# Three steps per head pair in place of four, with row maxima ahead of older steps' values, and filling counted over steps

## The chip, the cores and the metric

The kernel runs on one core of a Trainium2 chip. The time is that of one execution on the device, in microseconds; the time of a kernel is the median of several runs. One further execution is recorded by the hardware profiler, and every row of the profile comes from that one.

## The reference

A trunk of two layers on a sequence of S = 512 tokens, D = 1024. Layer 0 mixes with forgetting attention (FoX, 16 heads of 64), layer 1 with latent attention (MLA, 8 heads of 128 + 64 rotary), whose keys and values are computed once from the stream after layer 0. An MLP of width 4096 with a squared ReLU follows each, and a normalisation closes the trunk. All is float32. The two attentions share this causal softmax in blocks of 128 queries:

```python
def one_block(args):
    i, qb = args
    logits = logits_fn(qb)          # FoX: q.k*scale + cum_q - cum_k; MLA: nope part + rotary part
    qpos = i * Q_BLOCK + jnp.arange(Q_BLOCK)
    logits = jnp.where(kpos[None, :] <= qpos[:, None], logits, -jnp.inf)
    p = jax.nn.softmax(logits, axis=-1).astype(v.dtype)
    return jnp.einsum('bhqk,bkhd->bqhd', p, v)

x = x + ctx.reshape(B, S, W) @ w_out
x = x + sq_relu_mlp(rms_norm(x, norm_ffn_g[layer]), w_up, w_down)
```

## The kernel before

Every float32 operand is split into a rounded high part and a remainder, and each product is three matmuls (high·high, high·low, low·high; `three`, line 260). A weight piece of 512 KB comes by DMA on SP's queue (`fetch`), ScalarE (ACT) casts it to `whi`, VectorE (DVE) subtracts to `wlo` (`piece`, line 250: it prepares the piece asked for and the next one).

Both attentions go through `attention` (line 415). It takes two heads at a time: 8 pairs in FoX, 4 in MLA. A pair has four steps, one for each block of 128 queries, the longest first: blocks 3, 2, 1, 0 with 512, 384, 256 and 128 key columns. A step n does the following, in the order in which the code issues it.

- `start(p)` at a pair's first step: the pair's projection must have been issued; in FoX the table `nb` of forget sums for this pair is loaded on SP's queue (line 577).
- `scores` (line 587 for FoX, 1094 for MLA): TensorE writes the scores of the two heads to two `sc` banks. FoX heads have 64 rows each, so head 0 uses rows 0 to 63 and head 1 rows 64 to 127, and their matmuls alternate; MLA has three matmuls on 128 rows for each head and then three on 64 rows for each. In FoX DVE adds the causal mask to a 128-column part of `nb`.
- `soft_step` (line 379): DVE takes row maxima (a reduction that also writes the tile `t`), ACT the exponentials with their row sums, DVE a reciprocal and two multiplies.
- SKEW = 3 steps later the step's tiles are turned (`turn_unit`, line 405): TensorE transposes them to a `tp` bank, ACT copies to `pth`, DVE subtracts to `ptl`. After a pair's last step `values` multiplies with the values, head by head.
- `fill.run(12)` after each step (9 in MLA), and `fill.run(18)` between the values of the two heads (6 in MLA), hand out other matmuls for TensorE: the later pairs' projections (`proj`, line 499, to `acc` banks, then DVE `t<-acc,rstd`, ACT `r<-t`, DVE `r<-t,r`), the remaining values (`v4_gen`, line 561) and the beginning of the output projection (`out_begin`, line 451). The numbers are FILL1 and FILL2 (lines 34, 35); the Filler (line 347) draws pieces from generators until n are used up, and forgets what a piece took beyond n. `until(key)` draws all up to that piece.

In the attentions a scheduler at build time takes the instructions in about this order, each as its inputs and buffers allow, and writes one fixed sequence for each engine. In the MLPs the order is the written one. Nearly all instructions go through one helper, so the profile puts them on line 112; they are told apart by the names of their tiles.

## Time and profile before

| | us |
|---|---|
| median of 3 runs (1128.93 to 1130.05) | 1128.96 |
| profiled execution | 1129.98 |
| its span | 1127.8 |
| TensorE (PE) busy | 1112.5 |
| VectorE (DVE) busy | 778.8 |
| ScalarE (ACT) busy | 582.3 |

The span is the time from the first to the last recorded instruction. FoX's attention lies at about 52 to 234 us, MLA's at about 651 to 745 us of it; the MLPs between and behind them. A timeline row is the start, the length, engine, line, operation, output<-inputs, rows, then output<-input shapes and how many like it follow each other; in square brackets how long the engine was idle ahead and who released it. Matmuls overlap in the pipeline, so lengths add up to more than the time: from one start to the next is what counts. `MATMUL tp<-ident,t` are transposes, `sc<-r,r` scores, `tp<-pth,v` values, `acc<-r,whi` and `acc<-r,wlo` the filling. `CUSTOM_DVE_ANT_0 t<-sc,nb` is the reduction to row maxima.

### The profile page before, as it was taken

Reading aid. Unit: us, or ns where it says so; the run is one execution under the profiler, and the core shown is the slowest. Engines: PE = TensorE matmul, PEld = TensorE weight load, DVE = VectorE, ACT = ScalarE, POOL = GpSimd, SP = SyncE. Lnnn points to the kernel's source line nnn. Section 1 sums busy time; section 2 is a strip of 40 time slices with the busy share of each in tenths; the row PEclk is TensorE's granted clock in tenths of the full one; section 3 lists DMA queues with packets and bytes.
Section 4 is the critical chain, followed back from the end, with each engine's and each line's share of the span. In section 5 each row is a group of like instructions: output and inputs, shape, how many; then the busy total and the mean of one; then the engine's idle time right before and its main releaser. Section 6 shows DMA issues by size and latency. Waiting matters only on the chain.

```text
span 1127.8 us, 14208 instructions
## 1 busy us (share of the span) xinstructions
PE 1112.5 (99%) x5324; PEld 910.0 (81%) x5324; DVE 778.8 (69%) x1422; ACT 582.3 (52%) x1067; POOL 13.0 (1%) x46
## 2 busy tenths in 40 slices
PE   8999999999999999999999999999999999999997
PEld 6878887788888888888888877888888888888885
DVE  6897788765476667576896878736265765765784
ACT  5565565544555455434444767634575544444622
POOL 1000000001000000000000000000000000000000
PEclk9999999999999999999999999999999999999999
DMA  5423212133634415321345212213442511611402
GB/s 189 132 82 104 78 61 90 57 131 112 246 127 131 131 38 158 105 63 36 125 132 155 75 50 75 94 56 107 154 170 74 186 57 57 200 57 43 131 1 75
DMA packets 37109, 116.92 MB, mean 104 GB/s; under 512 B 4384, under 2 KB 5024, under 8 KB 37040
## 3 DMA queue, kind: packets, MB, share of 16 engines
q1 hardware_dynamic: 36176, 114.41, 31.1%
q10 hardware_dynamic: 864, 1.60, 0.4%
q8 instruction: 42, 0.69, 0.3%
q14 instruction: 27, 0.22, 0.1%
HBM read 109.67 MB, written 6.33 MB: 103 GB/s over the span
## 4 chain that ended last, share of the span: by engine, by line
PE 95%; DVE 2%; ACT 1%; DMA 1%; issue 0%; SPq 0%; ACTq 0%
PE up L112 35%; PE acc L112 20%; PE go L112 19%; PE sc L112 8%; PE tp L112 7%; PE keep L112 6%; DVE t L112 1%; ACT t L112 1%; DVE r L112 1%; DMA nb<-csc 0%; DMA t<-xT 0%; DVE wlo L112 0%; ACT whi L112 0%; ACT r L112 0%; DVE rs L112 0%
## 5 line engine op out<-in xcount | busy, mean ns | idle before, releaser
L112 PE MATMUL acc<-r,whi 128*128 128x512 f32 x606 | 197.2, 405 | 5.2 <-ACT whi L112 4.8
L112 PE MATMUL up<-r,r 128*128 128x512 f32 x808 | 192.5, 390 | 0.0
L112 PEld LDWEIGHTS up<-r,r 128*128 128x128 f32 x808 | 151.3, 188 | 31.6
L112 PE MATMUL up<-r,whi 128*128 128x512 f32 x544 | 170.7, 390 | 0.0
L112 DVE TENSOR_TENSOR wlo<-raw,whi 128x1024 fp32r<-128x1024 f32 (+3 forms) x95 | 111.3, 1171 | 44.6 <-ACT whi L112 43.8
L112 DVE TENSOR_TENSOR t<-s,t 128x512 fp32r<-128x512 f32 x84 | 57.8, 688 | 118.3 <-ACT t L112 118.2
L112 PEld LDWEIGHTS acc<-r,whi 128*128 128x128 f32 x606 | 111.5, 191 | 30.9 <-ACT whi L112 4.8
L112 ACT CAST whi<-raw 128x1024 fp32r<-128x1024 f32 (+3 forms) x95 | 95.5, 1008 | 77.7 <-PE acc L112 36.6
L112 ACT ACTIVATE s<-up 128x512 f32<-128x512 f32 x56 | 33.4, 597 | 183.5 <-PE up L112 183.5
L112 PE MATMUL acc<-r,wlo 128*128 128x512 f32 x303 | 119.9, 396 | 0.0
L112 PEld LDWEIGHTS up<-r,whi 128*128 128x128 f32 x544 | 101.8, 188 | 20.8
L112 PE MATMUL up<-r,wlo 128*128 128x512 f32 x288 | 112.1, 389 | 0.0
L112 PE MATMUL go<-r,t 128*128 128x512 f32 x360 | 86.5, 389 | 0.0
L112 PE MATMUL sc<-r,r 128*128 128x512 f32 (+7 forms) x480 | 79.9, 355 | 0.9 <-DVE sm L112 0.3
L112 PEld LDWEIGHTS go<-r,t 128*128 128x128 f32 x360 | 67.6, 188 | 14.0
L112 PE MATMUL go<-whi,t 128*128 128x512 f32 x240 | 78.7, 389 | 0.0
L112 PEld LDWEIGHTS sc<-r,r 64*128 64x128 f32 (+1 forms) x480 | 56.1, 186 | 23.6 <-issue 8.7
L112 PEld LDWEIGHTS acc<-r,wlo 128*128 128x128 f32 x303 | 57.6, 190 | 12.8 <-issue 0.4
L112 DVE TENSOR_TENSOR r<-raw,r 128x512 fp32r<-128x512 f32 x72 | 47.3, 696 | 24.2 <-ACT r L112 24.2
L112 PEld LDWEIGHTS up<-r,wlo 128*128 128x128 f32 x288 | 54.0, 188 | 11.3
L112 ACT ACTIVATE s<-s 128x512 f32<-128x512 f32 x64 | 40.5, 632 | 39.6 <-DVE s L112 37.8
L112 DVE TENSOR_TENSOR r<-q,r 128x512 fp32r<-128x512 f32 x94 | 60.4, 683 | 0.0
(201 smaller groups left out, 1848.7 us busy)
## 6 DMA issues: line engine op xcount, KB each, us to landing
raw<-wts SPq DMA_DIRECT2D x122, 512.0 KB, 3.6
q<-wts SPq DMA_DIRECT2D x56, 512.0 KB, 4.7
nb<-csc SPq DMA_DIRECT2D x8, 512.0 KB, 4.7
t<-xT SPq DMA_DIRECT2D x8, 256.0 KB, 6.2
r<-xT SPq DMA_DIRECT2D x8, 256.0 KB, 5.6
xmid<-r SPq DMA_DIRECT2D x8, 256.0 KB, 7.4
r<-xmid SPq DMA_DIRECT2D x8, 256.0 KB, 4.5
xkeep<-r SPq DMA_DIRECT2D x8, 256.0 KB, 2.1
```

What stands on the lines that cost most here:

```text
L112: ins = fn(*args, **kw)
```

## The change

Blocks 1 and 0 of a pair are one step: their scores lie side by side in the same two `sc` banks, their transposes in one `tp` bank, and one reciprocal serves the four columns of sums. So a pair has three steps. SKEW is 2. `soft_step` is cut in two: `row_maxima` is issued right behind the scores, and the exponentials, reciprocal and multiplies behind `values(..., 0)` and `turn(st, 0)` of an older step. The Filler carries over in `due` what a piece took too much; `v4`'s pieces count 3 each in place of 6; MLA hands out 12 in place of 9 per step. FoX score matmuls are tied to their written order by `behind(ins, other)`, which adds a dependency for the scheduler, the first of each step behind the last maxima issued (kind "Sync", a wait on the chip too), and mask additions behind the maxima too. In MLA the joined step runs block 1 as before (128-row matmuls, then 64-row) and block 0 the other way round. FoX contexts are split when a pair's values end instead of when the output projection asks; one more weight piece is prepared ahead just before each output projection; the last output column uses a `tp` bank. TensorE has as many matmuls as before, ACT as many instructions, and DVE 12 reciprocals fewer.

```diff
-SKEW = 3
+GROUPS = ((3,), (2,), (1, 0))
+SKEW = 2
 FILL1 = (12, 18)
-FILL2 = (9, 6)
+FILL2 = (12, 6)
...
+EARLIER = [[n for n, _ in PIECES].index(n) - 1 for n in ("fo", "mo")]
...
-        for j in (n, n + 1):
+        for j in range(n, n + 2 + (n in EARLIER)):
             if j not in state["ready"] and j < len(PIECES) and not order["on"]:
...
+            self.due = 0
         def add(self, key, gen):
             self.gens.append((key, gen))
         def run(self, n):
-            while n > 0 and self.gens:
+            self.due += n
+            while self.due > 0 and self.gens:
                 key, gen = self.gens[0]
                 c = next(gen, None)
                 if c is None:
                     self.gens.pop(0)
                     self.done.add(key)
                 else:
-                    n -= c
+                    self.due -= c
+            self.due = min(self.due, 0)
         def until(self, key):
             while key not in self.done:
+                self.due = 0
                 self.run(1)
...
+    maxima = {}
+    def places(blocks_):
+        o = 0
+        for i in blocks_:
+            yield i, slice(o, o + (i + 1) * P)
+            o += (i + 1) * P
+    def row_maxima(blocks_, scs, biases, factor=None):
+        k = 2 * len(blocks_)
+        m = small.tile([P, 4], F32, tag="sm0", name=nm("sm"), bufs=4)[:, :k]
         Ls = [tt(), tt()]
-        for e in range(2):
-            nc.vector.tensor_tensor_reduce(
-                out=Ls[e][:, :n], in0=scs[e][:, :n], in1=biases[e], scale=-1.0, scalar=3.4e38, op0=ALU.add, op1=ALU.min, accum_out=m[:, e : e + 1]
+        cols = [(i, c, e, 2 * n + e) for n, (i, c) in enumerate(places(blocks_)) for e in range(2)]
+        for i, c, e, a in cols:
+            ins = nc.vector.tensor_tensor_reduce(
+                out=Ls[e][:, c], in0=scs[e][:, c], in1=biases(i, e), scale=-1.0, scalar=3.4e38, op0=ALU.add, op1=ALU.min, accum_out=m[:, a : a + 1]
             )
+            maxima["last"] = ins.ins.name
...
+        return Ls, m, cols, factor
+    def soft_step(Ls, m, cols, factor):
+        rs, r = (small.tile([P, 4], F32, tag=f"sm{j}", name=nm("sm"), bufs=4)[:, : len(cols)] for j in (1, 2))
+        for i, c, e, a in cols:
             nc.scalar.activation(
-                out=Ls[e][:, :n],
-                in_=Ls[e][:, :n],
+                out=Ls[e][:, c],
+                in_=Ls[e][:, c],
                 func=AF.Exp,
-                scale=-1.0 if factor is None else factor,
-                bias=m[:, e : e + 1],
-                accum_out=rs[:, e : e + 1],
+                scale=-1.0 if factor is None else factor(i),
+                bias=m[:, a : a + 1],
+                accum_out=rs[:, a : a + 1],
             )
         nc.vector.reciprocal(r, rs)
-        for e in range(2):
-            nc.vector.tensor_scalar_mul(Ls[e][:, :n], Ls[e][:, :n], r[:, e : e + 1])
-        return Ls
-    def turn_unit(L, i, pth, ptl):
-        n = (i + 1) * P
+        for i, c, e, a in cols:
+            nc.vector.tensor_scalar_mul(Ls[e][:, c], Ls[e][:, c], r[:, a : a + 1])
+    def turn_unit(L, blocks_, pth, ptl):
         tp = bank("tp")
-        for j in range(i + 1):
-            nc.tensor.transpose(tp[:, j * P : (j + 1) * P], L[:, j * P : (j + 1) * P], ident)
-        src = tp[:, :n].rearrange("p (j q) -> p j q", q=P)
-        nc.scalar.copy(pth[:, i : 4 * i + 1 : 3, :], src)
-        nc.vector.tensor_tensor(ptl[:, i : 4 * i + 1 : 3, :], src, f32(pth[:, i : 4 * i + 1 : 3, :]), op=ALU.subtract)
+        for i, c in places(blocks_):
+            for o in range(c.start, c.stop, P):
+                nc.tensor.transpose(tp[:, o : o + P], L[:, o : o + P], ident)
+        for i, c in places(blocks_):
+            src = tp[:, c].rearrange("p (j q) -> p j q", q=P)
+            nc.scalar.copy(pth[:, i : 4 * i + 1 : 3, :], src)
+            nc.vector.tensor_tensor(ptl[:, i : 4 * i + 1 : 3, :], src, f32(pth[:, i : 4 * i + 1 : 3, :]), op=ALU.subtract)
     def attention(pairs, apool, start, scores, values, fill, per_step, out_gen):
...
-            p, i, Ls = st
+            p, g, Ls = st
-            turn_unit(Ls[e], i, *bufs[p, e])
-        steps = [(p, i) for p in range(pairs) for i in range(NB - 1, -1, -1)]
+            turn_unit(Ls[e], g, *bufs[p, e])
+        steps = [(p, g) for p in range(pairs) for g in GROUPS]
         ready = {}
         for n in range(len(steps) + SKEW + 1):
             if n < len(steps):
-                p, i = steps[n]
-                if i == NB - 1:
+                p, g = steps[n]
+                if g == GROUPS[0]:
                     start(p)
-                ready[n] = (p, i, soft_step(*scores(p, i)))
+                part = row_maxima(g, *scores(p, g))
+                ready[n] = (p, g, part[0])
             elif n == len(steps):
                 fill.add("out2", out_gen(["sc"] * 2))
             m = n - SKEW
             st = ready.pop(m, None)
-            done = (m - 1) // NB if m > 0 and m % NB == 0 else None
+            done = (m - 1) // len(GROUPS) if m > 0 and m % len(GROUPS) == 0 else None
             if done is not None:
                 values(done, 0, *bufs.pop((done, 0)))
             if st:
                 turn(st, 0)
+            if n < len(steps):
+                soft_step(*part)
             if done is not None:
                 fill.run(per_step[1] if n < len(steps) else 6)
                 values(done, 1, *bufs.pop((done, 1)))
...
-                        yield 6
+                        yield 3
                 value_parts(q, tb, pp)
-                yield 6
+                yield 3
...
-        def scores(p, i):
-            n = (i + 1) * P
-            q = slice(i * P, n)
+        def scores(p, blocks_):
             (qh, ql), (kh, kl) = qk[p]
             scs = [bank("sc"), bank("sc")]
-            for a, b2, st, sp in ((qh, kh, True, False), (qh, kl, False, False), (ql, kh, False, True)):
-                for e in range(2):
-                    rows = slice(e * FHD, (e + 1) * FHD)
-                    mm(scs[e][:, :n], a[rows, q], b2[rows, :n], start=st, stop=sp)
+            last = None
+            for i, c in places(blocks_):
+                n = (i + 1) * P
+                for a, b2, st, sp in ((qh, kh, True, False), (qh, kl, False, False), (ql, kh, False, True)):
+                    for e in range(2):
+                        rows = slice(e * FHD, (e + 1) * FHD)
+                        ins = mm(scs[e][:, c], a[rows, n - P : n], b2[rows, :n], start=st, stop=sp)
+                        if last:
+                            behind(ins, last)
+                        else:
+                            behind(ins, maxima.get("last"), "Sync")
+                        last = ins.ins.name
             nb = nbs[p]
             mask = maskz[:, S - P :].unsqueeze(1).to_broadcast([P, 2, P])
-            nc.vector.tensor_tensor(nb[:, :, q], nb[:, :, q], mask, op=ALU.add)
-            return scs, n, [nb[:, e, :n] for e in range(2)]
+            def bias(i, e):
+                n = (i + 1) * P
+                if e == 0:
+                    behind(nc.vector.tensor_tensor(nb[:, :, n - P : n], nb[:, :, n - P : n], mask, op=ALU.add), maxima.get("last"))
+                return nb[:, e, :n]
+            return scs, bias
...
-            whole[0] += e
-        whole = [0]
+            if e:
+                split_ctx(p)
...
-                op = bank("acc")
+                op = bank("acc" if f < KD - 1 else "tp")
...
-        def scores(p, i):
-            n = (i + 1) * P
-            q = slice(i * P, n)
+        def scores(p, blocks_):
             scs = [bank("sc"), bank("sc")]
             qrh, qrl = qr[p]
-            for e in range(2):
-                a, b2 = qn[2 * p + e], kn[2 * p + e]
-                three(scs[e][:, :n], a[0][:, q], a[1][:, q], b2[0][:, :n], b2[1][:, :n], True, False)
-            for a, b2, sp in ((qrh, krh, False), (qrh, krl, False), (qrl, krh, True)):
-                for e in range(2):
-                    rows = slice(e * ROPE, (e + 1) * ROPE)
-                    mm(scs[e][:, :n], a[rows, q], b2[rows, :n], start=False, stop=sp)
-            return scs, n, [maskz[:, S - n :]] * 2, rs_q[:, i : i + 1]
+            last = None
+            for i, c in places(blocks_):
+                n = (i + 1) * P
+                q = slice(n - P, n)
+                for turn in ((0, 1), (1, 0))[i != blocks_[0]]:
+                    if turn == 0:
+                        for e in range(2):
+                            a, b2 = qn[2 * p + e], kn[2 * p + e]
+                            three(scs[e][:, c], a[0][:, q], a[1][:, q], b2[0][:, :n], b2[1][:, :n], i == blocks_[0], i != blocks_[0])
+                    else:
+                        for k, (a, b2) in enumerate(((qrh, krh), (qrh, krl), (qrl, krh))):
+                            for e in range(2):
+                                rows = slice(e * ROPE, (e + 1) * ROPE)
...
+                                behind(ins, last)
+                                last = ins.ins.name
+            return scs, lambda i, e: maskz[:, S - (i + 1) * P :], lambda i: rs_q[:, i : i + 1]
```

On TensorE, the two short steps of FoX's third pair. `sc_1057`, `sc_1058` are the two heads' banks of block 1 and `sc_1098`, `sc_1099` those of block 0; `tp<-ident` are transposes. Before, the end of block 1's scores and what follows:

```order
L112 MATMUL sc_1058<-r_839,r_741 128x256
L112 MATMUL sc_1057<-r_838,r_742 128x256
L112 MATMUL sc_1058<-r_838,r_742 128x256
L112 MATMUL tp_1078<-ident,t_854 128x128
L112 MATMUL tp_1082<-ident,t_855 128x128
L112 MATMUL acc_1044<-r_137,whi_944 128x512
```

Twelve `acc` matmuls stand there, and then block 0:

```order
L112 MATMUL acc_1044<-r_149,wlo_945 128x512
L112 MATMUL sc_1098<-r_838,r_741 128x128
L112 MATMUL sc_1099<-r_838,r_741 128x128
L112 MATMUL sc_1098<-r_839,r_741 128x128
L112 MATMUL sc_1099<-r_839,r_741 128x128
L112 MATMUL sc_1098<-r_838,r_742 128x128
L112 MATMUL sc_1099<-r_838,r_742 128x128
L112 MATMUL tp_1120<-pth_875,v_469 128x512
```

After, with both blocks in `sc_1018` and `sc_1019`:

```order
L114 MATMUL sc_1018<-r_862,r_771 128x256
L114 MATMUL sc_1019<-r_862,r_771 128x256
L114 MATMUL sc_1018<-r_862,r_770 128x128
L114 MATMUL sc_1019<-r_862,r_770 128x128
L114 MATMUL sc_1018<-r_863,r_770 128x128
L114 MATMUL sc_1019<-r_863,r_770 128x128
L114 MATMUL sc_1018<-r_862,r_771 128x128
L114 MATMUL sc_1019<-r_862,r_771 128x128
L114 MATMUL tp_1042<-pth_822,v_469 128x512
```

The two transposes and twelve projection matmuls between the passes are gone from there; block 0's six stand directly behind block 1's, and then come values.

On DVE, between FoX's first and second pair. `t_607`, `t_608` (after: `t_610`, `t_611`) are the tiles of pair 0's block 1, and after of block 0 too; `acc_576` holds half of pair 1's projection; `ISA t<-sc,nb` is the reduction to row maxima. Before:

```order
L112 RECIPROCAL sm_606<-sm_605 128x2
L112 TENSOR_SCALAR t_607<-t_607,sm_606 128x256
L112 TENSOR_SCALAR t_608<-t_608,sm_606 128x256
L112 SCALAR_TENSOR_TENSOR t_628<-acc_576,rstd_291 128x512
L112 TENSOR_TENSOR wlo_780<-raw_777,whi_779 128x1024
L112 TENSOR_TENSOR r_631<-t_628,r_630 128x512
L112 ISA t_646,sm_643<-sc_634,nb_512 128x128
L112 ISA sm_643 128x1
L112 ISA t_647,sm_643<-sc_635,nb_512 128x128
L112 ISA sm_643 128x1
L112 TENSOR_TENSOR ptl_656<-tp_657,pth_655 128x4x128
L112 TENSOR_TENSOR ptl_665<-tp_666,pth_664 128x4x128
```

After:

```order
L114 ISA sm_609 128x1
L114 TENSOR_TENSOR ptl_619<-tp_620,pth_618 128x4x128
L114 TENSOR_TENSOR nb_514<-nb_514,maskz 128x2x128
L114 RECIPROCAL sm_628<-sm_627 128x4
L114 TENSOR_SCALAR t_610<-t_610,sm_628 128x256
L114 TENSOR_SCALAR t_611<-t_611,sm_628 128x256
L114 TENSOR_SCALAR t_610<-t_610,sm_628 128x128
L114 TENSOR_SCALAR t_611<-t_611,sm_628 128x128
L114 TENSOR_TENSOR ptl_639<-tp_640,pth_638 128x4x128
L114 SCALAR_TENSOR_TENSOR t_659<-acc_576,rstd_291 128x512
L114 TENSOR_TENSOR wlo_778<-raw_775,whi_777 128x1024
L114 TENSOR_TENSOR r_662<-t_659,r_661 128x512
```

`t<-acc_576` stood behind block 1's two multiplies and ahead of block 0's maxima and both `ptl`; now it stands behind the maxima of both blocks, their one reciprocal, four multiplies and two `ptl`.

On TensorE, the first scores of FoX's last pair, `sc_2372` and `sc_2373`. Before:

```order
L112 MATMUL tp_2345<-ident,t_2104 128x128 x4
L112 MATMUL sc_2372<-r_2283,r_2175 128x512
L112 MATMUL sc_2373<-r_2283,r_2175 128x512
L112 MATMUL tp_2393<-ident,t_2148 128x128 x3
L112 MATMUL sc_2372<-r_2284,r_2175 128x512
L112 MATMUL sc_2373<-r_2284,r_2175 128x512
L112 MATMUL sc_2372<-r_2283,r_2176 128x512
L112 MATMUL sc_2373<-r_2283,r_2176 128x512
L112 MATMUL tp_2399<-ident,t_2149 128x128 x3
L112 MATMUL tp_2438<-ident,t_2204 128x128 x2
L112 MATMUL acc_2287<-r_2312,whi_2182 128x512
```

After, where the pass is `sc_2300` and `sc_2301` and `acc_2270` a column of the output projection:

```order
L114 MATMUL acc_2270<-r_877,wlo_2157 128x512
L114 MATMUL acc_2270<-r_1115,whi_2156 128x512
L114 MATMUL acc_2270<-r_1116,whi_2156 128x512
L114 MATMUL acc_2270<-r_1115,wlo_2157 128x512
L114 MATMUL sc_2300<-r_2241,r_2143 128x512
L114 MATMUL sc_2301<-r_2241,r_2143 128x512
L114 MATMUL sc_2300<-r_2242,r_2143 128x512
L114 MATMUL sc_2301<-r_2242,r_2143 128x512
L114 MATMUL sc_2300<-r_2241,r_2144 128x512
L114 MATMUL sc_2301<-r_2241,r_2144 128x512
L114 MATMUL tp_2314<-ident,t_2107 128x128 x3
```

In before the pass is cut by transposes and no filling stands in front of it; now twelve `acc` matmuls, of which the last four are shown, stand ahead of it, and it is in one piece.

31 lines of the change are left out of this document (20 added, 11 removed).

## The prediction

> **What bounds the kernel now.** I read the page first, then the windows, then TensorE's waits, then single stretches of the timeline.
>
> ```profile
> PE 1112.5 (99%) x5324; PEld 910.0 (81%) x5324; DVE 778.8 (69%) x1422; ACT 582.3 (52%) x1067; POOL 13.0 (1%) x46
> PE 95%; DVE 2%; ACT 1%; DMA 1%; issue 0%; SPq 0%; ACTq 0%
> ```
>
> TensorE (PE) is busy for 99% of the span, and 95% of the chain that ended last runs on it. The same matmuls remain after the change, so only two things can move the time: the gaps in PE's stream, and the edges at which a short group of matmuls costs more than its columns. The windows show how little lies in plain gaps.
>
> ```profile
> 52.15:234.00 181.85, 180.47 (x1069) 145.00 (x1067) 148.19 (x403) 107.30 (x260) 0.00 (x0) 1.00 0.24 78
> 260.00:600.00 340.00, 340.00 (x1525) 282.03 (x1525) 229.99 (x311) 161.94 (x255) 3.30 (x13) 1.00 0.36 117
> 684.00:702.00 18.00, 17.85 (x96) 13.98 (x95) 14.99 (x36) 12.88 (x28) 0.00 (x0) 1.00 0.29 98
> ```
>
> The longest waits of PE (engine, tile, line, who released it, us in total, times, longest):
>
> ```profile
> PE acc L112 <- ACT whi L112: 4.8, 1, 4.8
> PE tp L112 <- DVE ptl L112: 0.9, 1, 0.9
> PE sc L112 <- DVE r L112: 0.4, 2, 0.2
> ```
>
> The columns of the windows are start and end, length, then busy time of PE, weight load, DVE, ACT and POOL, and the granted clock, 1.00 throughout. In the MLP (260 to 600) PE has no gap at all, 340.00 of 340.00, and 340.00 / 1525 = 0.223 us is what a 512-column matmul takes in a stream. The FoX attention has 181.85 − 180.47 = 1.38 us of gap, a stretch of the MLA attention 0.15. The longest wait is at the start of the program, which the change leaves alone. DVE is 148.19 / 181.85 = 81% busy in FoX, so it can be late but is no bound. Gaps are not all: modelled ends hide part of a wait, so below I go by the starts of matmuls and 0.23 us for one of 512 columns.
>
> **The change, part by part. Joined short steps.** In the trace of before the two short steps of a FoX pair look like this:
>
> ```profile
> 99.66 0.62 PE L112 MATMUL sc<-r,r 64*128 64x256 f32 x6
> 100.21 0.44 PE L112 MATMUL tp<-ident,t 128*128 128x128 f32 x2
> 100.40 0.71 PE L112 MATMUL acc<-r,whi 128*128 128x512 f32 x2
> 100.95 0.40 PE L112 MATMUL acc<-r,wlo 128*128 128x512 f32 x1
> ...
> 103.03 0.39 PE L112 MATMUL acc<-r,wlo 128*128 128x512 f32 x1
> 103.34 0.55 PE L112 MATMUL sc<-r,r 64*128 64x128 f32 x6
> 103.83 0.50 PE L112 MATMUL tp<-pth,v 128*128 128x512 f32 x1
> ```
>
> Six score matmuls of 256 columns take 100.21 − 99.66 = 0.55 us, six of 128 take 103.83 − 103.34 = 0.49. Half the columns save only 0.06, so much of a short pass is edge. The six are three pairs, a head on each half of the 128 rows, so three slots: 0.223 × 256 / 512 = 0.11 us each for 256 columns, and for 128 columns about the same, as eight transposes of 128 columns take 0.85 us in a row further down, 0.11 each. Joined, I take one pass to cost 0.55 + 3 × 0.11 = 0.88 against 0.55 + 0.49 = 1.04: 0.16 less. The entry into the second pass goes too: 103.03 to 103.34 is 0.31 where 0.23 is the stream, 0.08. The two transposes of block 1 no longer stand alone, so one return to 512-column matmuls goes: two matmuls from 100.40 to 100.95 are 0.55 instead of 0.46, 0.09. Together 0.33, of which I count 0.30, as PE sometimes enters a pass from transposes and not from projections. Bounds: 0.16 (the pass alone) to 0.45 (the second pass costs its 64-row columns alone, 3 × 0.06, in place of 0.33). Eight pairs: **−2.4 us** (−1.3 to −3.6).
>
> ```profile
> 706.80 1.42 PE L112 MATMUL sc<-r,r 128*128 128x256 f32 x12
> 708.15 0.44 PE L112 MATMUL tp<-ident,t 128*128 128x128 f32 x2
> ...
> 711.18 1.26 PE L112 MATMUL sc<-r,r 128*128 128x128 f32 x12
> 712.37 0.50 PE L112 MATMUL tp<-pth,r 128*128 128x512 f32 x1
> ```
>
> In MLA the passes take 708.15 − 706.80 = 1.35 and 712.37 − 711.18 = 1.19, 2.54 together. The new order inside the joined pass (block 1 full rows then half rows, block 0 half rows then full rows) leaves out one crossing each way, so I take 18 matmul slots (twelve full-row, six side by side pairs) of 0.11 and two crossings of 0.1: about 2.2. With 0.09 for the transposes as above, 0.4 per pair; bounds 0.2 to 0.6. Four pairs: **−1.6 us** (−0.8 to −2.4).
>
> All of this saves edges. The Trainium skill, "TensorEngine Tiling (Array Packing)", section "Key Properties", says that a change of the tiling mode, not of the tile alone, drains TensorE. The trace agrees in direction (0.49 for a pass whose columns need a third of 0.55's). By that rule alone I would count two crossings fewer per pair at 0.08 each, an estimate of 12 × 0.16 = 1.9 us in place of 4.0, and the sum at the end would be 2.1 us higher.
>
> **The end of FoX.** Here the work that is handed out between the steps has run out:
>
> ```profile
> 203.37 0.55 PE L112 MATMUL tp<-ident,t 128*128 128x128 f32 x3
> 204.10 0.73 PE L112 MATMUL sc<-r,r 64*128 64x512 f32 x4 [0.19 <-DVE r L112]
> 204.83 0.55 PE L112 MATMUL tp<-ident,t 128*128 128x128 f32 x3
> 206.27 0.44 PE L112 MATMUL tp<-ident,t 128*128 128x128 f32 x2 [0.90 <-DVE ptl L112]
> 206.47 0.96 PE L112 MATMUL acc<-r,whi 128*128 128x512 f32 x3
> ```
>
> From 203.37 to 206.47 are 3.10 us. Eight transposes at 0.11 and four side by side score matmuls (two lengths of 0.23, entry 0.1) are 1.4; so 1.7 is waiting, and the pass cut in two has an entry and an exit more (0.08 + 0.09, on both sides 0.3). In the order of after 12 `acc` matmuls stand ahead of this pass, 12 × 0.23 = 2.8 us, longer than the wait: **−2.0 us** (−1.0 to −2.3). What is late next is DVE's maxima of this pass, which have the transposes and the next filling in front of them.
>
> **Between the first two FoX pairs** the order puts a new wait. TensorE in before, then the two others:
>
> ```profile
> 60.22 0.62 PE L112 MATMUL sc<-r,r 64*128 64x256 f32 x6
> 64.23 1.09 PE L112 MATMUL tp<-ident,t 128*128 128x128 f32 x8
> 65.08 0.72 PE L112 MATMUL acc<-r,whi 128*128 128x512 f32 x2
> ```
>
> DVE and ACT in the same stretch:
>
> ```profile
> 62.45 0.42 DVE L112 CUSTOM_DVE_ANT_0 t<-sc,nb 128x256 f32<-128x256 f32 x1
> 64.77 0.68 DVE L112 SCALAR_TENSOR_TENSOR t<-acc,rstd 128x512 f32<-128x512 f32 x1
> 67.10 0.28 DVE L112 CUSTOM_DVE_ANT_0 t<-sc,nb 128x128 f32<-128x128 f32 x1
> 67.52 1.28 DVE L112 TENSOR_TENSOR ptl<-tp,pth 128x512 fp32r<-128x512 f32 x2
> 62.90 0.51 ACT L112 ACTIVATE t<-t,sm 128x256 f32<-128x256 f32 x1 [2.35 <-DVE sm L112]
> 65.48 0.62 ACT L112 CAST r<-t 128x512 fp32r<-128x512 f32 x1 [0.55 <-DVE t L112]
> ```
>
> `t<-acc,rstd` takes the second half of pair 1's projection (the keys or queries that its first scores need); ACT casts it to `r`. In before it starts at 64.77 and two 256-column multiplies are all that stand near it. In after it stands behind both blocks' maxima, one reciprocal that needs all four exponentials, four multiplies and two `ptl`. From the same 62.45, with 0.08 of overlap taken off a row (two 128-column maxima: 67.52 − 67.10 = 0.42 for two rows of 0.28): two maxima 0.68, mask 0.34, two maxima 0.42, `ptl` 0.60, next mask 0.34 give 64.8; the last exponential ends near 65.3; reciprocal 0.1, multiplies 2 × 0.27 + 2 × 0.20, `ptl` 0.60, `t<-acc` 0.60 end at 67.5, the cast at 68.1. PE: joined pass 60.22 + 0.88 = 61.1, eight transposes 65.08 − 64.23 = 0.85, 12 and 6 projection matmuls 18 × 0.23 = 4.2, six transposes 0.75 with their edge, one more 0.23: at the scores by 67.1. So it waits 1.0; the pass is then split in two with projections between (0.3, as above), and the lower half of `r` is behind a weight subtraction (0.2): **+1.5 us**. Queued behind the waiting matmul is all of PE. Bounds: 0 (DVE is ahead of this count) and 4.0 (the wait repeats in part at two later pairs).
>
> **MLA's waits.** The first pair of MLA waits for DVE:
>
> ```profile
> 662.15 0.61 PE L112 MATMUL acc<-r,whi 128*128 128x512 f32 x2
> 663.04 1.16 PE L112 MATMUL sc<-r,r 128*128 128x256 f32 x6 [0.28 <-DVE sm L112]
> 664.13 0.50 PE L112 MATMUL acc<-r,wlo 128*128 128x512 f32 x1
> ```
>
> Two matmuls start at 662.15, the next group 0.89 later instead of 0.46: 0.43. The half pass behind it, one head alone, takes 664.13 − 663.04 = 1.09 where half of the whole pass of 1.35 is 0.68: 0.41 of edges. With maxima issued ahead of older values and turning, and one pass less, I take −0.5 here, and another −0.5 for the gaps from 684 on (0.15 above, and the passes cut there), as 12 matmuls now follow each step instead of 9: **−1.0 us** (0 to −2.2).
>
> **Costed at nothing.** Twelve reciprocals fewer, on a DVE with 181.85 − 148.19 = 33.7 us free in FoX. Contexts split as they come: the same ACT and DVE rows, spread; without the cover they would show once, at most 0.7 + 0.6 per pair. One weight piece earlier before each output projection: its cast and subtraction move ahead by a piece, behind 18 projection matmuls. The last output column in another bank: no wait stands there in before. The order that ties the first score matmul behind the last maxima: these now come directly behind their scores, with 2.8 us of filling between; with no filling it would cost two maxima, 1.2 us, once per such step. The mask additions no longer stand on DVE in front of the maxima while their table arrives on SP's queue; that frees DVE, not PE. The projections of pairs 5 and 6 end just in time after the change; before it one does:
>
> ```profile
> 185.07 0.50 PE L112 MATMUL sc<-r,r 64*128 64x512 f32 x2 [0.23 <-ACT r L112]
> ```
>
> The wait of 0.23 and a pass cut in two (0.3) come once more or not: 0, ±0.5.
>
> **Sum.** −2.4 − 1.6 − 2.0 + 1.5 − 1.0 = −5.5 us. The profiled execution was 1129.98 us (its span 1127.8 and 2.2 around it), so it would be 1124.5. The median of the runs is 1.0 below that execution: **1123.5 us**.
>
> **The rivals.** *The waits only move.* DVE and ACT do the same work per pair, and if PE stays just behind them each wait removed returns a step later. For it speaks DVE's 81%; against it that PE's gaps in FoX were 1.4 us only, so PE is behind DVE nearly everywhere. Then −4.0 + 1.5 = −2.5: 1126.5. *No new wait and no old one.* If DVE reaches `t<-acc` by 67.1, the +1.5 goes and MLA loses the 2.2 of its upper bound: −2.4 − 1.6 − 2.0 − 2.2 = −8.2, 1120.8. *Slower: every pair's first scores wait like pair 1's.* Mechanism: the projection of a pair ends in the last filling before its scores, and DVE takes it only after reciprocal, multiplies and `ptl` of the joined step. At 1.5 us a pair the change costs −7.0 + 1.5 n, slower from n = 5 on; at all seven boundaries +3.5, 1132.5. For it: 3 × 12 + 18 = 54 matmuls per pair are asked for now, 4 × 12 + 18 = 66 before, so projections end later. Against: the groups of `v4` count 3 each instead of 6, so more come per step, and in the order the later pairs' projections end a step or more ahead, except at 5 and 6.
>
> **How the numbers follow.** Forecast 0.52, waits that move 0.20, no wait 0.17, slower 0.11. The forecast with its bounds reaches from 1121 to 1127; the range takes in the case without waits and 1.8 below it (edges at their bound), and the waits that move and 2.0 above them (a smaller saving of edges): 1119.0 to 1128.5. It leaves out the slower case. A measurement of this kernel tells 0.2% (2.3 us) from no change: faster means below 1126.7, slower above 1131.2. The forecast is nearly all on the faster side, the first rival half: faster 0.75, same 0.16, slower 0.09.
>
> **What would show it.** Joined passes of FoX near 0.88 and of MLA near 2.2 us; no stretch in the last FoX pair where transposes and scores alone alternate over 3 us; one wait of the score matmuls for `r` of about 1 us near 67; windows of FoX 3 us shorter, of MLA 2.5 us shorter, MLP windows alike. Wrong would be: a wait at each pair's first scores, a joined pass of over 1.0 us, or an attention window with PE's gaps as large as before.

## The result and the profile after

The changed kernel takes 1121.48 us (median of 4 runs, 1121.28 to 1122.23); the kernel before takes 1129.22 in the same comparison (1128.93 to 1130.05). The ratio is 0.9931, interval 0.9919 to 0.9943: faster by 0.7%, or 7.7 us. The forecast was 1123.5, or 5.5 us.

The profiled execution took 1121.28 us with a span of 1119.1. The page of the changed kernel, its busy times and the engines on its last chain:

```profile
PE 1103.1 (99%) x5324; PEld 907.2 (81%) x5324; DVE 778.3 (70%) x1410; ACT 582.1 (52%) x1067; POOL 13.1 (1%) x46
...
PE 94%; DVE 3%; ACT 2%; DMA 0%; issue 0%; SPq 0%; DVEq 0%; ACTq 0%
```

TensorE is still what bounds the kernel, with 1112.5 − 1103.1 = 9.4 us less busy time for the same 5324 matmuls. So busy time was not all streaming: edges between short groups, parts of waits and the slower first microseconds (last section) are counted as busy. Where it went is read from three windows per kernel: from the first FoX score matmul to the first matmul of the MLP, that MLP, and from the first MLA score matmul to the second MLP. Before, then after (start and end, length, busy PE, weight load, DVE, ACT, POOL, granted clock, DMA):

```profile
52.72:262.09 209.37, 207.99 (x1189) 167.85 (x1189) 167.50 (x429) 121.30 (x280) 0.00 (x0) 1.00 0.27 90
262.09:587.42 325.33, 325.33 (x1457) 269.86 (x1455) 218.21 (x293) 156.03 (x246) 3.30 (x13) 1.00 0.36 116
647.67:782.68 135.01, 134.41 (x708) 108.26 (x708) 92.23 (x232) 74.16 (x162) 1.97 (x9) 1.00 0.24 75
```

```profile
51.41:255.82 204.41, 203.53 (x1189) 167.47 (x1189) 168.31 (x421) 121.26 (x280) 0.00 (x0) 1.00 0.29 92
255.82:581.15 325.33, 325.33 (x1456) 269.93 (x1455) 218.26 (x293) 156.08 (x246) 3.44 (x13) 1.00 0.35 116
641.44:773.95 132.51, 130.90 (x707) 107.13 (x708) 90.63 (x228) 73.65 (x162) 1.97 (x9) 1.00 0.24 77
```

FoX is 209.37 − 204.41 = 4.96 us shorter, MLA 135.01 − 132.51 = 2.50, and the MLP equal to the hundredth. Together 7.46, which is the difference of the medians but for 0.3. The rest of the profiles' difference (their spans are 8.7 apart) lies ahead of FoX, whose first score comes 52.72 − 51.41 = 1.31 earlier behind the same instructions; the last section comes back to it. Below, FoX and MLA always mean these two windows; they repeat to about 0.1 us where a kernel's instructions there are the same.

The waits of TensorE after:

```profile
PE acc L114 <- ACT whi L114: 4.9, 1, 4.9
PE tp L114 <- DVE r L114: 1.4, 1, 1.4
PE sc L114 <- ACT r L114: 0.9, 1, 0.9
```

The wait `tp <- DVE ptl` of 0.9 is gone; `sc <- ACT r` of 0.9, at pair 1, is the one that was forecast; `tp <- DVE r` of 1.4 is new and was not. The timeline of TensorE after, at a joined FoX pass, a joined MLA pass, the last FoX pair, and the two new waits:

```profile
94.67 0.39 PE L114 MATMUL acc<-r,wlo 128*128 128x512 f32 x1
94.99 0.90 PE L114 MATMUL sc<-r,r 64*128 64x256 f32 x12
95.82 0.50 PE L114 MATMUL tp<-pth,v 128*128 128x512 f32 x1
...
673.87 2.57 PE L114 MATMUL sc<-r,r 128*128 128x256 f32 x24
676.27 0.44 PE L114 MATMUL tp<-pth,r 128*128 128x512 f32 x1
676.56 0.40 PE L114 MATMUL tp<-ptl,r 128*128 128x512 f32 x1
...
202.71 0.39 PE L114 MATMUL acc<-r,wlo 128*128 128x512 f32 x1
203.03 0.97 PE L114 MATMUL sc<-r,r 64*128 64x512 f32 x6
203.93 0.88 PE L114 MATMUL tp<-ident,t 128*128 128x128 f32 x6
204.56 0.71 PE L114 MATMUL acc<-r,whi 128*128 128x512 f32 x2
...
65.38 0.48 PE L114 MATMUL acc<-r,whi 128*128 128x512 f32 x1
66.72 0.50 PE L114 MATMUL sc<-r,r 64*128 64x512 f32 x2 [0.87 <-ACT r L114]
...
682.45 0.27 PE L114 MATMUL tp<-pth,r 128*128 128x128 f32 x1
684.10 0.65 PE L114 MATMUL tp<-ident,t 128*128 128x128 f32 x4 [1.37 <-DVE r L114]
```

A joined FoX pass takes 95.82 − 94.99 = 0.83 us (forecast 0.88; 1.04 apart), one of MLA 676.27 − 673.87 = 2.40 (forecast 2.2; 2.54 apart). In the last pair the scores stand in one piece, with matmuls of the output projection in front and, behind the transposes, again.

### The profile page after: what moved, and what is told of

The parts are those of the page before. It is cut to its first block, busy times and chain, and to the rows that moved or that the text cites. A ratio compares the mean times of both kernels' runs of the same rounds, so it can differ in the third digit from the quotient of the medians.

```text
span 1119.1 us, 14201 instructions
## 1 busy us (share of the span) xinstructions
PE 1103.1 (99%) x5324; PEld 907.2 (81%) x5324; DVE 778.3 (70%) x1410; ACT 582.1 (52%) x1067; POOL 13.1 (1%) x46
## 4 chain that ended last, share of the span: by engine, by line
PE 94%; DVE 3%; ACT 2%; DMA 0%; issue 0%; SPq 0%; DVEq 0%; ACTq 0%
PE up L114 35%; PE go L114 19%; PE acc L114 19%; PE tp L114 8%; PE sc L114 7%; PE keep L114 6%; DVE t L114 2%; ACT t L114 1%; DVE r L114 1%; DMA t<-xT 0%; DVE wlo L114 0%; ACT r L114 0%; DVE rs L114 0%; DVE fs L114 0%; DVE sm L114 0%
## 5 line engine op out<-in xcount | busy, mean ns | idle before, releaser
L114 PE MATMUL acc<-r,whi 128*128 128x512 f32 x574 | 184.9, 402 | 5.1 <-ACT whi L114 4.9
L114 PEld LDWEIGHTS acc<-r,whi 128*128 128x128 f32 x574 | 105.0, 189 | 29.0 <-ACT whi L114 5.2
L114 PE MATMUL acc<-r,wlo 128*128 128x512 f32 x287 | 112.8, 393 | 0.1
L114 PE MATMUL sc<-r,r 128*128 128x512 f32 (+6 forms) x480 | 74.6, 350 | 1.1 <-ACT r L114 0.9
L114 PEld LDWEIGHTS sc<-r,r 64*128 64x128 f32 (+1 forms) x480 | 53.7, 186 | 20.2 <-issue 5.8
L114 PEld LDWEIGHTS acc<-r,wlo 128*128 128x128 f32 x287 | 54.2, 189 | 12.1 <-DVE wlo L114 0.4
```

What stands on the lines that cost most here:

```text
L114: ins = fn(*args, **kw)
```

## The experiments

Each result gives the median of the kernel and, from its trace, the lengths of FoX and MLA. The kernel before was timed beside each group; its medians there were 1129.46, 1129.14 and 1129.41.

| kernel | median, us | FoX | MLA |
|---|---|---|---|
| before | 1129.22 | 209.4 | 135.0 |
| after | 1121.48 | 204.4 | 132.5 |
| four_steps | 1128.76 | 207.2 | 136.7 |
| four_nine | 1129.39 | 208.0 | 136.8 |
| three_16 | 1123.63 | 206.4 | 132.5 |
| soft_together | 1124.64 | 204.6 | 134.8 |
| front_fill | 1121.14 | 201.2 | 132.6 |
| mla_cross | 1121.69 | 204.4 | 132.8 |
| small_ones | 1125.53 | 208.5 | 132.6 |
| four_soft | 1129.30 | 207.3 | 137.5 |
| late_split | 1125.64 | 208.4 | 132.6 |
| no_earlier | 1121.53 | 204.4 | 132.6 |
| before_split | 1126.48 | 206.7 | 135.1 |
| mla_9_18 | 1122.13 | 204.4 | 133.4 |

**Four steps again (four_steps).**

```diff
-GROUPS = ((3,), (2,), (1, 0))
-SKEW = 2
+GROUPS = ((3,), (2,), (1,), (0,))
+SKEW = 3
-FILL2 = (12, 6)
+FILL2 = (9, 6)
```

> The changed kernel with four steps per pair again (SKEW 3, 12 matmuls of filling per step in FoX, 9 in MLA); all else of the change stays. Theory 'edges' (a pass and a turn fewer per pair, 0.35 us in FoX and 0.3 in MLA): 4.0 us of it come back. Theory 'filling' (fewer matmuls asked for per pair leave some for the last one): 66 per pair are asked for again, so FoX's last pair waits again, +3. Pair 1's wait of 1.1 goes, since the projection ends a step earlier. Together +6: 1127.5. If the order of maxima, values and turning made the gain, it stays: 1121.5.

1128.76 us (1128.49 to 1129.5), ratio to before 0.9995, interval 0.9986 to 1.0004. Without the joined step the whole change is worth nothing. But it is a sum: FoX is 2.2 us shorter than before, MLA 136.7 − 135.0 = 1.7 longer. The order of the maxima alone does not carry the gain. In FoX it is 2.8 longer than after, where 'edges' and 'filling' together asked for 2.8 + 3 less pair 1's 1.1; so one of the two is smaller than it was taken. In this kernel, too, the end has little filling: its waits in FoX, 0.5 for `DVE r` and 0.5 for `DVE ptl`, both come behind the last pair's scores, at 222.6 and 223.7. In MLA its plain waits add up to 1.8 us, against 0.3 in before.

**Four steps with less filling (four_nine).** As above, and

```diff
-FILL1 = (12, 18)
+FILL1 = (9, 18)
```

> As the kernel with four steps, but 9 matmuls of filling per FoX step, so 54 per pair as with three steps. 'Edges': +4.0 stays, 1125.5, and the last FoX pair has its filling, no alternation of transposes and scores there. 'Filling' alone: as the changed kernel, 1121.5.

1129.39 us (1128.82 to 1130.22). FoX is 208.0 − 204.4 = 3.6 us longer than after. Here the two kernels hand out as many matmuls per pair, both have filling in the last pair and both a wait at pair 1 (0.4 and 0.9), so this is nearest to the price of the edges alone: 3.6 / 8 = 0.45 us per FoX pair, where 0.30 was taken. 'Filling' alone had asked for no loss and falls; but with four steps, fewer matmuls per step did not help either: FoX is 0.8 longer than in four_steps.

**Three steps with more filling (three_16).**

```diff
-FILL1 = (12, 18)
+FILL1 = (16, 18)
```

> The changed kernel with 16 instead of 12 matmuls of filling per FoX step, so three steps but 66 per pair. 'Filling': nothing is left for the last FoX pair, +3.0 there; pair 1's projection ends a step earlier and its wait of 1.1 goes: 1123.4. 'Edges' alone: no loss at the end, 1120.4.

1123.63 us (1123.43 to 1123.79), FoX 2.0 longer than after, MLA the same. Filling can run out. The longest waits are now these:

```profile
PE tp L114 <- DVE r L114: 3.1, 5, 1.3
PE sc L114 <- DVE sm L114: 1.1, 2, 0.9
```

Of the five waits for a `tp` bank the longest, 1.3, is MLA's, as in after. The other four, 1.7 us together, are new. They stand from 208 us on, with FoX's last two pairs, where nothing is left between the values of two heads. So the number matters. 'Filling' met its 1123.4 by two errors that nearly cancel: the end lost 2.0 and not 3.0, and pair 1's wait did not go; it is now `sc <- DVE sm`, 0.9. Beside four_steps, which asks for 66 matmuls per pair as well, FoX is only 207.2 − 206.4 = 0.8 shorter; but three_16 has 2.8 us of plain waits in FoX and four_steps 1.0. With that difference of 1.8 put back, the joined step is worth 2.6, or 0.33 per pair.

**Exponentials directly behind the maxima (soft_together).**

```diff
                 ready[n] = (p, g, part[0])
+                soft_step(*part)
...
-            if n < len(steps):
-                soft_step(*part)
```

> The changed kernel with exponentials, reciprocal and multiplies issued directly behind the row maxima, ahead of older steps' values and turning, as before the change. TensorE's order stays; only DVE and ACT have another. If the order of maxima earns something, values and turning wait for DVE's reciprocal and multiplies again: +1 to +2 us, seen as waits of transposes for tp banks. By 'edges' and 'filling': within 0.5 of 1121.5.

1124.64 us (1123.05 to 1125.1). TensorE's order is the same; FoX is 0.2 longer, MLA 2.3. Its waits:

```profile
PE tp L114 <- DVE r L114: 3.4, 3, 1.5
PE sc L114 <- ACT r L114: 0.9, 1, 0.9
```

The wait for a `tp` bank comes three times, once with the values of each of the first three MLA pairs, instead of once. At the second DVE reads:

```profile
708.93 0.18 DVE L114 RECIPROCAL sm<-sm 128x4 f32<-128x4 f32 x1 [2.23 <-ACT t L114]
709.14 1.01 DVE L114 TENSOR_SCALAR t<-t,sm 128x256 f32<-128x256 f32 x4
710.06 0.69 DVE L114 TENSOR_TENSOR r<-tp,r 128x512 fp32r<-128x512 f32 x1
```

`r<-tp,r` frees the bank. It stands behind a reciprocal that waits 2.23 for four exponentials, and behind four multiplies; TensorE's transposes start at 710.80 after 1.55 of waiting. In after that subtraction comes first. In MLA the new order is worth 2.3 us (two of the three waits, 1.5 and 0.5, are gone in after), in FoX nothing that counts.

**Pair 1's projection earlier (front_fill).**

```diff
-        fill.run(12)
+        fill.run(24)
```

> The changed kernel with 24 instead of 12 matmuls of filling ahead of FoX's first scores. Theory: pair 1's first scores wait because its projection ends just ahead of them; it now ends 12 matmuls earlier, the wait (1.1 us at 65.4) and the cut of that pass (0.3) go: 1120.2. Rival: DVE is late whatever the place of the projection, the wait only changes its name: 1121.5.

1121.14 us (1120.79 to 1121.67), ratio 0.9929 (0.9915 to 0.9944) beside after's 0.9931: no difference that can be told. Twelve matmuls (2.7 us) moved ahead of the window, so FoX is 201.2 + 2.7 = 203.9, at most 0.5 shorter. The waits of TensorE now:

```profile
PE tp L114 <- DVE r L114: 1.4, 1, 1.4
PE sc L114 <- DVE sm L114: 1.1, 1, 1.1
```

The rival was right: `sc <- ACT r` is gone and the same score matmuls wait 1.1 for the last maxima of the step before. They have two grounds to: the tie that the change put there, and the two `sc` banks, which those maxima are the last to read (FoX has no others). DVE, busy for 8.03 of the 8.50 us from 60.1 to 68.6, is late there, whatever it is that it is waited for.

**Block 0 of MLA in block 1's order (mla_cross).**

```diff
-                for turn in ((0, 1), (1, 0))[i != blocks_[0]]:
+                for turn in (0, 1):
...
-                            three(scs[e][:, c], a[0][:, q], a[1][:, q], b2[0][:, :n], b2[1][:, :n], i == blocks_[0], i != blocks_[0])
+                            three(scs[e][:, c], a[0][:, q], a[1][:, q], b2[0][:, :n], b2[1][:, :n], True, False)
...
```

The flags that start and end a sum in a bank follow the order; the second half of that is left out here.

> The changed kernel with block 0 of MLA's joined step in block 1's order (128-row matmuls, then 64-row), so two crossings more inside each of the four passes. If a crossing has a price of its own (a drain), a pass goes from 2.36 to 2.54 us as in the two passes of before, +0.7 us: 1122.2. If only the start and end of a pass cost, 2.36 stays and the time too: 1121.5.

1121.69 us (1121.29 to 1122.34), MLA only 0.25 longer. In its timeline:

```profile
674.46 2.72 PE L114 MATMUL sc<-r,r 128*128 128x256 f32 x24
677.10 0.50 PE L114 MATMUL tp<-pth,r 128*128 128x512 f32 x1
...
683.37 0.27 PE L114 MATMUL tp<-pth,r 128*128 128x128 f32 x1
684.03 0.66 PE L114 MATMUL tp<-ident,t 128*128 128x128 f32 x4 [0.39 <-DVE r L114]
```

The pass takes 677.10 − 674.46 = 2.64 instead of 2.40: two crossings more, one inside the pass and one at its end, 0.12 each. At the next pair it takes 702.11 − 699.46 = 2.65 instead of 701.86 − 699.50 = 2.36, 0.14 each. Four passes make +1.0 to +1.2. But the wait behind the pass shown shrinks from 1.37 to 0.39 (1.0 less), since TensorE arrives later at a bank that DVE frees at the same time. So most of what the turned order saves is given back to that wait in the changed kernel. And at 2.64 the joined pass is no shorter than the two of before (2.54): in MLA it is the turned order of block 0, not the joining, that shortens the pass itself.

**Three small parts undone (small_ones)**: no piece earlier, the last column in an `acc` bank, and

```diff
-            if e:
-                split_ctx(p)
+            whole[0] += e
+
+        whole = [0]
...
-            return out_begin("fo", tags, outs, lambda: len(parts), lambda k: parts[k])
+            return out_begin("fo", tags, outs, lambda: whole[0], ctx_part)
...
```

`ctx_part(k)` splits context k when a matmul of the output projection first asks for it, as in the kernel before.

> The changed kernel with three parts undone: no weight piece earlier, the last output column in an acc bank, FoX contexts split when the output projection asks. The prediction costed them at nothing: within 0.5 of 1121.5, FoX and MLA stretches alike. If they earn something, up to +2 at the ends of the two attentions.

1125.53 us (1125.11 to 1126.82): what was costed at nothing is worth 208.5 − 204.4 = 4.1 us in FoX. The next three runs take it apart.

**Contexts split late, alone (late_split)**: the diff above without the two other parts.

> The changed kernel with one part undone: FoX contexts are split when the output projection asks. Theory 'ready': the last pair waited in before, not because too many matmuls were asked for, but because the output projection's inputs, the split contexts, were not there, so that filling could not be placed; then this alone gives FoX its 4.1 us back that the three small parts gave together: 1125.5. Rival: the weight piece ahead or the other bank did it: 1121.5.

1125.64 us (1125.31 to 1126.46), FoX 4.0 longer than after. Of the 4.1 that the three parts gave together, nearly all is the splitting. In the timeline of this kernel the stretch of before is back, with three steps and 54 matmuls asked for per pair:

```profile
201.76 0.50 PE L114 MATMUL sc<-r,r 64*128 64x512 f32 x2
202.19 0.55 PE L114 MATMUL tp<-ident,t 128*128 128x128 f32 x3
202.84 0.73 PE L114 MATMUL sc<-r,r 64*128 64x512 f32 x4
203.56 0.55 PE L114 MATMUL tp<-ident,t 128*128 128x128 f32 x3
204.29 0.55 PE L114 MATMUL tp<-ident,t 128*128 128x128 f32 x3 [0.18 <-DVE ptl L114]
205.81 0.97 PE L114 MATMUL acc<-r,whi 128*128 128x512 f32 x3 [0.98 <-ACT r L114]
```

The last row names the cause: an output projection matmul, which is filling, waits 0.98 for ACT's `r`, the cast of a context. The filling was asked for, but its inputs were not made.

**No piece earlier, alone (no_earlier).**

```diff
-EARLIER = [[n for n, _ in PIECES].index(n) - 1 for n in ("fo", "mo")]
+EARLIER = [[n for n, _ in PIECES].index(n) - 1 for n in ()]
```

> The changed kernel without the weight piece prepared one earlier ahead of each output projection. 'Ready': within 0.5 of 1121.5. Rival: the weights, not the contexts, were late: up to +4.1, 1125.5.

1121.53 us (1121.18 to 1121.72), FoX and MLA as after: worth nothing. The other bank was not tried alone; 0.1 us is left for it.

**The kernel before with contexts split early (before_split).**

```diff
-            whole[0] += e
-
-        whole = [0]
+            if e:
+                split_ctx(p)
+
...
-            return out_begin("fo", tags, outs, lambda: whole[0], ctx_part)
+            return out_begin("fo", tags, outs, lambda: len(parts), lambda k: parts[k])
...
```

> The kernel before with one part of the change: FoX contexts split when a pair's values end. 'Ready': the stretch of the last pair in which transposes and scores alternate goes, FoX 2 to 2.5 us shorter, 1127.0, with four steps and 66 matmuls asked for per pair. Theory 'filling': nothing is left for the last pair all the same, 1129.2.

1126.48 us (1125.73 to 1127.77), ratio 0.9976 (0.9967 to 0.9986). FoX is 209.4 − 206.7 = 2.6 us shorter by this one edit, with four steps and 66 matmuls per pair. Twelve filling matmuls now stand ahead of the last pair's first scores, of which the last is shown:

```profile
207.54 0.39 PE L112 MATMUL acc<-r,wlo 128*128 128x512 f32 x1
207.86 0.97 PE L112 MATMUL sc<-r,r 64*128 64x512 f32 x6
208.76 0.88 PE L112 MATMUL tp<-ident,t 128*128 128x128 f32 x6
```

**More filling between two heads' values in MLA (mla_9_18).**

```diff
-FILL2 = (12, 6)
+FILL2 = (9, 18)
```

> The changed kernel with 9 matmuls of filling per MLA step and 18 between the values of a pair's two heads (12 and 6). In MLA transposes wait 1.4 us at 684 for a tp bank that DVE frees late; 18 matmuls ahead of the second head's values, 9 more than now, are 2.0 us of cover: the wait goes, 1120.1. If DVE is behind by more, or the wait moves to the next pair: 1121.5.

1122.13 us (1121.8 to 1122.65), MLA 0.9 longer. The wait for the `tp` bank at 684 is gone, and a new one, on DVE's `r`, stands at the next pair's scores, whose projection now ends later:

```profile
688.99 1.72 PE L114 MATMUL sc<-r,r 128*128 128x512 f32 x6
691.39 1.38 PE L114 MATMUL sc<-r,r 128*128 128x512 f32 x6 [0.68 <-DVE r L114]
```

Two shorter waits for DVE's maxima, 0.5 together, come with it. The wait moved on, as the second guess had it.

**Four steps with exponentials directly behind the maxima (four_soft)**: the edits of four_steps and soft_together together.

> Four steps per pair as in the first experiment, and exponentials directly behind the maxima again, so that of the change only the filling's balance, the tied orders and the small parts stay. With four steps MLA took 1.7 us longer than before the change. If the new order of the maxima is what costs there, that comes back: 1127.0. If the order earns its 2.3 us in MLA whatever the number of steps: 1131. If the filling's balance is to blame: 1128.8, as without this edit.

1129.30 us (1128.65 to 1129.92), FoX as four_steps, MLA 137.5. The two kernels with four steps can't be told apart by their runs (1128.49 to 1129.50 for four_steps), and undoing the order brings nothing back; so the new order is not what makes MLA slower with four steps. Whether it earns something there is open. MLA is 137.5 − 136.7 = 0.8 longer than in four_steps, but this one execution was held up by the clock. In a window of 3.5 us in the middle of MLA the granted clock, third from the end, is 0.51:

```profile
685.50:689.00 3.50, 3.50 (x16) 3.36 (x15) 2.65 (x10) 1.41 (x7) 0.00 (x0) 0.51 0.30 82
```

The same matmuls, values of one head and four transposes, go from 685.25 to 688.86 here, 3.61 us, and from 685.49 to 687.60 in four_steps, 2.11. That is 1.5 us more, and a wait of 0.6 that four_steps has behind them does not come. The 0.8 is the difference of these two and no measure of the order. What makes MLA slower with four steps is not settled either: the filling's balance and the tied score matmuls stay in this kernel, and neither was tried alone.

## Why the prediction was right, and where it was not

The sign, the place and the order of size were right: FoX and MLA shorter, the MLPs the same, the cases apart by what TensorE waits for. Of 7.5 us in the two windows 5.5 were forecast; MLA came out at −2.5 where −2.6 was said, FoX at −5.0 where −2.9 was said.

*Joined short steps, FoX, −2.4: right mechanism, too small.* Four_nine puts it at 3.6, 0.45 per pair, at the far end of the bounds, and three_16 beside four_steps at 2.6, once their waits are evened out. The rows after lie between: a pass saves 1.04 − 0.83 = 0.21, not 0.16, and with the entry of 0.08 and the return of 0.09 as taken that is 0.38 per pair, 3.0 us. The pass was costed 0.05 too long, and 0.33 was rounded to 0.30.

*Joined short steps, MLA, −1.6: right mechanism, somewhat too large.* The pass saves 2.54 − 2.40 = 0.14 where 0.34 was taken, a return from transposes 0.09 as before: 0.23 per pair, 0.9 us. The price of a crossing was taken at 0.1 and is 0.12 to 0.14 by mla_cross. The 18 slots were taken too short: 2.40 less two crossings of 0.12 is 2.16, or 0.12 each with the edges of the pass. The rule of the Trainium skill, "TensorEngine Tiling (Array Packing)", section "Key Properties", that a change of tiling mode drains TensorE, gives no price; that each crossing costs time in mla_cross agrees with it. The 1.9 us that it alone gave for both attentions are less than the 3.0 + 0.9 of the rows. (Where the prediction says that the columns of the 0.49 pass need a third of 0.55's, they are half as many.)

*The end of FoX, −2.0: the size about right, the cause wrong.* This is the step that failed: "the work that is handed out between the steps has run out". It had not. Before_split keeps four steps and 66 matmuls per pair and gains 2.6 us by one edit, and late_split brings the stretch back with three steps and 54. The filling there is the output projection, whose matmuls read the split contexts: a high part that ACT casts, and a low part that DVE subtracts. ACT (the first row) and DVE in the kernel before:

```profile
205.79 0.62 ACT L112 CAST r<-r 128x512 fp32r<-128x512 f32 x1
204.08 0.69 DVE L112 TENSOR_TENSOR r<-r,tp 64x512 f32<-64x512 f32 x1
204.80 0.69 DVE L112 TENSOR_TENSOR r<-raw,r 128x512 fp32r<-128x512 f32 x1
205.53 0.69 DVE L112 TENSOR_TENSOR ptl<-tp,pth 128x512 fp32r<-128x512 f32 x1
...
207.34 0.69 DVE L112 TENSOR_TENSOR r<-r,r 128x512 fp32r<-128x512 f32 x1
```

No context is split before these: ACT's first cast of one runs from 205.79 to 206.41, DVE's first low part, `r<-r,r`, begins at 207.34. Both come behind the last scores of the pass (204.10 to 204.83), so nothing that reads them can stand ahead of it; the output projection goes on at 206.47, just behind the cast. In after the eight low parts begin at 86, 106, 127, 152, 178, 203, 222 and 230 us, so five stand ready when the last pair's pass comes at 203.03. The prediction saw 0.90 of waiting for `ptl` and read it as nothing left to do. It followed that "contexts split as they come" was costed at nothing, though that edit is worth 4.0 us in the changed kernel, of 7.5 in both windows, and 2.6 in the one before. That −2.0 came out near is luck: the change held the edit that mattered beside the one that was named. The two effects meet: three_16 shows that with too much asked for per step the filling does run out, 2.0 us. In before the splits also come all at once, six on ACT and DVE from 206 to 214 us, and crowd both engines there. The same edit undoes this too, and no run tells the two effects apart.

*The wait at pair 1, +1.5: right.* 0.87 of wait with 0.25 of edge around it (65.38 to 66.72 is 1.34 where 0.23 is the stream, so 1.1), and the pass cut in two (0.3): 1.4. But front_fill shows that the named cause, the place of `t<-acc` on DVE, is one of several: with the projection earlier the maxima are late by the same 1.1. DVE is busy for 6.76 of the 7.00 us from 60 to 67 in after. That its amount of work there sets the wait fits both, but no run made it less. With −3.0 to −3.6 for the joined steps, −2.6 for the end and +1.4 here, FoX's terms add up to −4.2 to −4.8 of its −5.0.

*MLA's waits, −1.0: right in place, too small.* With 0.9 for the edges, 2.5 − 0.9 = 1.6 is left. Most of it shows at the places that were named, the passes that were cut or held up: the short passes of the first pair go from 663.04 to 667.76 in before, 4.72 with what cuts them, and from 656.81 to 660.06 in after, 3.25, and block 0's pass of the second pair took 688.42 − 686.52 = 1.90 in before, 0.71 more than the 1.19 of the later pairs. One wait that no step named, 1.37 for a `tp` bank behind DVE's subtraction, gave part back. The order of the maxima, which the prediction put in half a sentence, carries 2.3 us there with three steps: without it that wait stands at all three boundaries.

*The rivals.* That the waits only move was too dark for the whole, but it is what the last improvements met: front_fill, mla_9_18 and mla_cross each moved a wait by the microsecond that they saved or cost. That each pair's first scores wait (slower) did not come: pair 1 alone does. That the old waits go without a new one fell by pair 1 and by MLA's 1.37, though its 1120.8 is nearer to the 1121.48 than the forecast is.

What each part is worth depends on the others: with four steps all the rest of the change gives FoX 2.2 and costs MLA 1.7, so that nothing is left; with three steps undoing the splits alone costs 4.0. The carry-over in `due`, the halved counts of `v4` and the tied orders were not undone one by one, so what each is worth is not shown. No version tried is faster than the changed kernel by more than can be told.

## What to carry to other kernels

Before a stretch without filling is put down to too little work, ask whether the work that is there had its inputs: the matmul that ends the stretch, and what released it, names them. An edit that only moves an operand's preparation earlier adds no work to its own engine, and can still decide where the scheduler may place the matmuls that read it. Where one engine is a microsecond behind, an edit to the order can change the name of the wait and not its length, so compare lengths of whole stretches between kernels, not single waits. And look at the granted clock of a stretch before its length is put down to the order: in four_soft 1.5 us were the clock's.

## What the runs showed of the hardware

The first matmuls run at about half rate, and when that ends differs between executions. TensorE in the window from 9 to 11 us, before, then after:

```profile
9.00:11.00 2.00, 2.00 (x5) 1.32 (x5) 2.00 (x4) 2.00 (x4) 0.00 (x0) 1.00 1.01 372
```

```profile
9.00:11.00 2.00, 1.80 (x8) 0.80 (x6) 2.00 (x4) 2.00 (x4) 0.00 (x0) 1.00 1.05 403
```

Five 512-column matmuls in 2 us against eight, with TensorE idle for 0.2 us at most. In before they start 0.43 us apart from 9.83 to 13.25 and, from 13.5 on, 0.23 apart; in after the first 0.23 comes at 8.94. The windows give the granted clock as 1.00 in both, but they average what is recorded, and the trace's own record of it begins, at full clock, only at 13.29 us of the span in before and at 8.75 in after. So it is the clock. It was at full rate 8.45 us after the first matmul (4.84) in before and 3.81 us after it (4.94) in after. Those two are the ends of what the fourteen profiles show.

The instructions there are the same in the two kernels, and soft_together, which has after's instructions up to FoX, has full clock at 12.69 and its first FoX score at 52.78, like before, not at 51.41. In the changed kernel and the seven of its variants that have the same matmuls in the same order up to there, the first score comes between 51.41 and 52.78. So the 1.3 us are chance between two executions, about the spread of a kernel's runs (1128.44 to 1130.24 for before). The Trainium skill, "TensorE: Matmul & The Clock Gate", section "What's actually happening", tells of an idle array at half clock and a free-running window of 3.4 us after which it is raised; the half rate and the 3.81 us of after agree, while its 0.5 us for how far the moment of it varies is less than the 4.64 us between the two seen here. A difference of 1 us between two profiles is therefore read from windows that leave the first 13 us out.

The clock can also fall back in the middle: the 3.5 us at 0.51 in four_soft cost 1.5 us. It is the only one of the fourteen profiles whose record has such a stretch ahead of the kernel's last microseconds.
